# Two blocks of a hybrid network on one core: the rotary turns of an indexer's queries by transfers within SBUF instead of matrix products

## The chip, the cores and the metric

The kernel runs on one core of one Trainium2 chip. The metric is device microseconds (us) of one execution. Five engines work side by side, each through its own instructions in a fixed order: TensorE (PE; its weight loads are listed apart as PEld), VectorE (DVE), ScalarE (ACT), GpSimd (POOL) and SyncE (SP). SP and ACT also start transfers (DMA); the part of an engine that does so is its queue (SPq, ACTq).

## The reference

A sequence of 512 tokens of width 1024 passes through two blocks of two layers each. The change lies in the second block, in both of its layers. There a latent of 256 columns is expanded twice: to 8 attention heads, and to 8 heads of a small "indexer" that decides which 128 of the keys each query may attend to. What the change touches is the rotary turn of the indexer's queries:

```python
def rope(x, positions):
    ...
    x1, x2 = jnp.split(x.astype(jnp.float32), 2, axis=-1)
    return jnp.concatenate([x1 * cos - x2 * sin, x2 * cos + x1 * sin], axis=-1).astype(x.dtype)
...
q_idx = rope((cq @ w_qidx_up).reshape(b_, seq, N_IDX_HEADS, IDX_DIM), positions)
...
idx_logits = jnp.einsum('thd,sd->ths', qib, ki32)
idx_score = jnp.einsum('ths,th->ts', jax.nn.relu(idx_logits), wib)
...
_, sel = lax.top_k(idx_score, n_sel)
```

Beside this attention a layer has a second mixer, an mLSTM with four heads, whose queries and keys go through a short convolution and whose output is gated.

## The kernel before

Activations lie transposed in SBUF: 128 features on the partitions, 512 tokens in a row. Two heads of 64 fill one tile, so the eight indexer heads are four tiles, p = 0 to 3. A rotary turn needs for every partition the value of the partner 32 rows away. `rope2` gets it in one of two ways: by a product with a 128x128 permutation (`swap`) into a PSUM bank `T`, or, when `swap` is None, by four transfers of 32 partitions each (64 KB) from tile to tile, which ACT's queue starts. Then DVE multiplies the partner by the sine (L1270), the tile by the cosine (L1271) and adds (L1275, or L1273 where there is a single output). The attention's own queries and keys (L1527 to L1539) already go by transfers in this kernel. For the indexer's queries the sum is split into a rounded part (ACT, L273) and the rest (DVE, L274), and both feed the score products.

The general products run with weights that are split the same way: a weight unit is loaded from HBM into a `wraw` buffer (L199), ACT casts it to `whi` (L273), DVE makes `wlo` (L274); there are three buffers of each. Product results are in the tiles `mm` (three banks), scores in `S` (two banks).

The stage around the change is the middle of `mixers2`. In program order:
- four times: six products of the latent with `wq` into an `mm` bank (`up`), an ACT copy to a tile `g` (L1382), and the rotary turn;
- the gates of the mLSTM: a chain of small ACT and DVE operations (L1392 to L1409) with two changes of ACT's function table;
- for p = 0 to 3 and three blocks of queries: six score products into two `S` banks, ACT's Relu out of each bank (L1425), and DVE's weighted sum (L1427, L1429). That is 24 Relus a layer;
- the mLSTM loop over four heads (L1459 to L1505), with DVE's top-k (L1284, L1285) in small steps between.

Between these stand jobs: the units of the short convolution (`conv`: 24 products of a weight unit with `h_lat`, then L1340, L1343, L1344). The order on each engine is not that of the program text: a scheduler orders each engine's instructions at build time, by priorities in program order and by its own estimate of when operands are ready. So an operation that it takes to be late lets others pass in front of it, on every engine. At run time each engine keeps this order.

Of the kernel before, what the change touches and what calls it, by code (L numbers as in the profile page):

```python
# [86 lines left out]
class Kern:  # L87
# [1201 lines left out]
    def mixers2(self, l, st, h, gw, cont):  # L1289
# [9 lines left out]
        g = lambda: self.til(G, [P, T], F32, "g")  # L1299
# [59 lines left out]
        def up(w, p):  # L1359
            ps = self.mmbank()  # L1360
            for k in range(2):
                c = slice((2 * p + k) * P, (2 * p + k + 1) * P)
                self.mm3(ps, w[0][:, c], w[1][:, c], cqn[k][0], cqn[k][1], k == 0, k == 1)
            return ps
# [15 lines left out]
        for p in range(4):  # L1380
            x = g()
            A.copy(x, up(wq, p))  # L1382
            q = hl()
            self.rope2(q, x, self.swap, g)
            iq.append(q)

        self.table()
# [24 lines left out]
        for p in range(4):  # L1412
            q = iq[p]
# [45 lines left out]
        for hd in range(4):  # L1459
# [4 lines left out]
            q, k = [self.need(j) for j in j_qk[hd]]  # L1464
# [669 lines left out]
```

## Time and profile before

| | |
|---|---|
| median of 3 runs | 3306.04 us (3303.74 to 3310.87) |
| profiled execution | 3315.37 us, of which the trace spans 3313.6 us |
| PE busy | 3171.0 us, 96% of the span |
| DVE, ACT busy | 2017.3 us (61%), 1355.8 us (41%) |
| granted PE clock, mean | 0.98 |
| the changed stage, layer 0 of block 2 | starts about 1900 us into the span |
| the same stage, layer 1 | starts about 2634 us |

Busy shares are means over the whole span. Inside a stage the engines take other shares, so the stage has to be read by itself. A busy PE in this trace counts a product from its start to its modelled end, and products overlap; how much of PE's time one product takes is read from the starts of the products around it.

### The profile page before, as it was taken

Reading aid. Unit: us, or ns where it says so; the run is one execution under the profiler, and the core shown is the slowest. Engines: PE = TensorE matmul, PEld = TensorE weight load, DVE = VectorE, ACT = ScalarE, POOL = GpSimd, SP = SyncE. Lnnn points to the kernel's source line nnn. Section 1 sums busy time; section 2 is a strip of 40 time slices with the busy share of each in tenths; the row PEclk is TensorE's granted clock in tenths of the full one; section 3 lists DMA queues with packets and bytes.
Section 4 is the critical chain, followed back from the end, with each engine's and each line's share of the span. In section 5 each row is a group of like instructions: output and inputs, shape, how many; then the busy total and the mean of one; then the engine's idle time right before and its main releaser. Section 6 shows DMA issues by size and latency. Waiting matters only on the chain. (4 is left out here: it accounts for less than half of the span.)

```text
span 3313.6 us, 52576 instructions
## 1 busy us (share of the span) xinstructions
PE 3171.0 (96%) x20868; PEld 2697.4 (81%) x20868; DVE 2017.3 (61%) x4147; ACT 1355.8 (41%) x2397; POOL 64.5 (2%) x91
## 2 busy tenths in 40 slices
PE   7899999999999899989999999989999999999999
PEld 5787778888889877778889968778889867778889
DVE  4757557544345756576665798575656797563335
ACT  4554454212122543443224575543325474543334
POOL 0000001000000000010000000000000000000000
PEclk9999999999999999999999999989999999999999
DMA  7443213324243422125554312245655212233235
GB/s 269 161 160 98 72 51 102 115 89 136 75 138 110 134 71 74 50 90 183 198 187 159 124 52 83 71 147 165 205 166 180 96 61 76 75 109 97 101 112 159
DMA packets 141925, 397.43 MB, mean 120 GB/s; under 512 B 29416, under 2 KB 39400, under 8 KB 141680
## 3 DMA queue, kind: packets, MB, share of 16 engines
q1 hardware_dynamic: 137440, 387.76, 36.0%
q10 hardware_dynamic: 4240, 6.31, 0.7%
q8 instruction: 164, 2.69, 0.3%
q14 instruction: 81, 0.66, 0.1%
HBM read 387.70 MB, written 2.11 MB: 118 GB/s over the span
## 5 line engine op out<-in xcount | busy, mean ns | idle before, releaser
L274 DVE TENSOR_TENSOR wlo<-wraw,whi 128x1024 fp32r<-128x1024 f32 (+3 forms) x484 | 568.0, 1177 | 661.8 <-PE mm L81 403.3
L81 PE MATMUL mm<-h_lat,whi 128*128 128x512 f32 (+1 forms) x3888 | 939.9, 387 | 2.1 <-DVE h_lat L368 0.9
L81 PEld LDWEIGHTS mm<-h_lat,whi 128*128 128x128 f32 x3888 | 715.4, 188 | 156.5 <-issue 14.3
L273 ACT CAST whi<-wraw 128x1024 fp32r<-128x1024 f32 (+3 forms) x484 | 488.0, 1013 | 853.7 <-PE mm L81 735.8
L81 PE MATMUL mm<-h_lat,wlo 128*128 128x512 f32 (+1 forms) x1944 | 491.6, 384 | 0.0
L81 PEld LDWEIGHTS mm<-h_lat,wlo 128*128 128x128 f32 x1944 | 363.5, 188 | 72.7 <-issue 2.9
L449 DVE SCALAR_TENSOR_TENSOR macc<-mraw,cst,macc 128x512 f32<-128x512 f32 x280 | 207.2, 750 | 36.3 <-DMA mraw<-wm 32.1
L81 PE MATMUL mm<-ah,whi 128*128 128x256 f32 (+1 forms) x702 | 217.5, 310 | 4.1 <-ACT hc L367 4.1
L81 PE MATMUL mm<-al,whi 128*128 128x256 f32 (+1 forms) x702 | 217.3, 310 | 0.0
L81 PE MATMUL mm<-ah,wlo 128*128 128x256 f32 (+1 forms) x702 | 217.2, 309 | 0.0
L81 PE MATMUL mm<-b,whi 128*128 128x256 f32 (+1 forms) x924 | 181.9, 295 | 0.0
L506 ACT ACTIVATE sb<-sb,least 128x512 f32<-128x512 f32 (+4 forms) x184 | 119.0, 647 | 110.3 <-DVE least L503 100.1
L81 PEld LDWEIGHTS mm<-b,whi 128*128 128x128 f32 x924 | 145.1, 188 | 6.0
L81 PEld LDWEIGHTS mm<-ah,whi 128*128 128x128 f32 x702 | 132.8, 189 | 11.8 <-ACT hc L367 4.2
L81 PEld LDWEIGHTS mm<-ah,wlo 128*128 128x128 f32 x702 | 132.9, 189 | 8.1
L81 PEld LDWEIGHTS mm<-al,whi 128*128 128x128 f32 x702 | 132.8, 189 | 7.4
L81 PE MATMUL mm<-b,wlo 128*128 128x256 f32 (+1 forms) x462 | 136.2, 295 | 0.0
L273 ACT CAST ah<-fx 128x256 fp32r<-128x256 f32 (+1 forms) x77 | 43.0, 559 | 199.3 <-DVE fx L1152 199.3
L81 PE MATMUL mm<-whi,h_lat 128*128 128x256 f32 x640 | 120.5, 289 | 1.8 <-DVE vm L274 1.8
L81 PE MATMUL S<-hc,whi 128*128 128x256 f32 (+1 forms) x768 | 107.5, 283 | 3.9 <-ACT whi L273 3.9
L81 PEld LDWEIGHTS mm<-whi,h_lat 128*128 128x128 f32 x640 | 102.4, 195 | 6.8 <-DVE vm L274 2.4
L81 PE MATMUL S<-h_lat,whi 128*128 128x256 f32 (+1 forms) x448 | 95.7, 302 | 9.4 <-ACT h_lat L367 5.3
(373 smaller groups left out, 5214.9 us busy)
## 6 DMA issues: line engine op xcount, KB each, us to landing
mraw<-wm SPq DMA_DIRECT2D x144, 512.0 KB
wraw<-wgu SPq DMA_DIRECT2D x88, 512.0 KB
wraw<-wgub SPq DMA_DIRECT2D x88, 512.0 KB
wraw<-wA SPq DMA_DIRECT2D x78, 512.0 KB
wraw<-wB SPq DMA_DIRECT2D x54, 512.0 KB
wraw<-wdb SPq DMA_DIRECT2D x56, 448.0 KB
wraw<-wm SPq DMA_DIRECT2D x48, 512.0 KB
wraw<-wd SPq DMA_DIRECT2D x44, 448.0 KB
```

What stands on the lines that cost most here:

```text
L81: return self.tell(self.K.nc.tensor.matmul(*a, **k))
L273: nc.scalar.copy(hi, ps)
L274: nc.vector.tensor_tensor(lo, ps, f32(hi), op=ALU.subtract)
L449: V.scalar_tensor_tensor(acc[v], raw[:, i * 512:(i + 1) * 512], c, acc[v], ALU.mult, ALU.add)
L506: A.activation(x["sb"], x["sb"], AF.Exp, bias=x["init"], scale=-1.0, accum_out=x["sum"])
```

## The change

In the loop over the indexer's four query tiles the argument that chooses the permutation product becomes None, so that the four transfers are made instead. It acts on eight turns: four tiles in each of two layers. The turn of the indexer's key (`swapdup`) stays a product.

```diff
--- before
+++ after
@@ -1381,7 +1381,7 @@
             x = g()
             A.copy(x, up(wq, p))
             q = hl()
-            self.rope2(q, x, self.swap, g)
+            self.rope2(q, x, None, g)
             iq.append(q)
```

With `swap` None the product's place is taken by these lines of `rope2`, and the cosine product is written over the tile itself instead of into a third one:

```python
            for i in range(4):
                j = i ^ 1
                nc.scalar.dma_start(u[32 * i:32 * i + 32], x[32 * j:32 * j + 32])
            pr, w = u, x
```

The scheduler gives a new order. Three places, all in layer 0; layer 1 has the same sequences.

The first is ACT's queue where the turns begin, in the kernel before. COPY is L1382 (tile g from an `up` bank), `kidx` the key's cast, `qh` the cast of a turned query tile, `whi` the cast of a weight unit.

```order
L1382 COPY g_19262<-mm_19263 128x512
L273 CAST kidx_19235<-g_19239 128x512
L1382 COPY g_19282<-mm_19283 128x512
L273 CAST qh_19271<-g_19275 128x512
L273 CAST whi_19651<-wraw_19650 128x1024
L1382 COPY g_19302<-mm_19303 128x512
```

And ACT's queue at the same place with the change:

```order
L1382 COPY g_19262<-mm_19263 128x512
L1265 DMA g_19273<-g_19262 32x512 x2
L273 CAST kidx_19235<-g_19239 128x512
L1265 DMA g_19273<-g_19262 32x512 x2
L273 CAST whi_19655<-wraw_19654 128x1024
L1382 COPY g_19283<-mm_19284 128x512
L1265 DMA g_19294<-g_19283 32x512 x4
L273 CAST qh_19271<-g_19262 128x512
L1382 COPY g_19304<-mm_19305 128x512
L273 CAST whi_19720<-wraw_19719 128x1024
```

The second COPY has moved behind four transfers and behind the cast of a weight unit.

The second place is ACT's queue at the first Relus out of the score banks (L1425), before; L1394 and L1395 are the gate chain's Exp and Ln, ACT_TABLE_LOAD changes the function table.

```order
L273 CAST qh_19331<-g_19335 128x512
L462 ACT_TABLE_LOAD
L1394 ACTIVATE g_19345<-g_19345 4x512
L1425 ACTIVATE g_19372<-S_19364 128x256
L1395 ACTIVATE g_19345<-g_19345 4x512
L1425 ACTIVATE g_19375<-S_19365 128x256
L1425 ACTIVATE g_19386<-S_19378 128x384
L273 CAST whi_19848<-wraw_19847 128x1024
```

With the change, ACT, the same two Relus (S_19368 and S_19369):

```order
L1425 ACTIVATE g_19376<-S_19368 128x256
L273 CAST whi_19917<-wraw_19916 128x1024
L1394 ACT_TABLE_LOAD
L1394 ACTIVATE g_19349<-g_19349 4x512
L273 CAST qh_19334<-g_19325 128x512
L462 ACT_TABLE_LOAD
L1395 ACTIVATE g_19349<-g_19349 4x512
L1425 ACTIVATE g_19379<-S_19369 128x256
L1425 ACTIVATE g_19390<-S_19382 128x384
```

Between the first and the second Relu there are now a weight cast, two table loads, Exp, Ln and the cast of the last query tile; before there was Ln alone.

The third place is PE's queue at the second block of scores. Before, `mm_19495` is the second conv unit of the stage (one of 16 products with `whi`, in the middle of which scores stand), and S the scores:

```order
L81 MATMUL mm_19495<-h_lat_87,whi_19490 128x512
L81 MATMUL S_19378<-kidx_19235,qh_19271 128x384
L81 MATMUL S_19378<-kidx_19236,qh_19271 128x384
L81 MATMUL S_19378<-kidx_19235,qh_19272 128x384
L81 MATMUL mm_19495<-h_lat_88,whi_19490 128x512
L81 MATMUL S_19379<-kidx_19235,qh_19271 128x384
```

With the change, PE, the same scores, now in the third conv unit, `mm_19660`:

```order
L81 MATMUL mm_19660<-h_lat_88,whi_19655 128x512
L81 MATMUL mm_19660<-h_lat_87,wlo_19656 128x512 x2
L81 MATMUL S_19382<-kidx_19235,qh_19271 128x384
L81 MATMUL S_19382<-kidx_19236,qh_19271 128x384
L81 MATMUL S_19382<-kidx_19235,qh_19272 128x384
L81 MATMUL mm_19660<-h_lat_87,wlo_19656 128x512 x6
L81 MATMUL S_19383<-kidx_19235,qh_19271 128x384
```

PE has a whole conv unit more in front of these scores. When it reaches the mLSTM's first products, 50 conv products of this stage are left in its queue; before, 58 were.

## Rows read from the trace of the kernel before

**Rows 1.** The page, part 1: busy time, share of the span, instructions.
```profile
PE 3171.0 (96%) x20868; PEld 2697.4 (81%) x20868; DVE 2017.3 (61%) x4147; ACT 1355.8 (41%) x2397; POOL 64.5 (2%) x91
```

**Rows 2.** Busy time by stretch of layer 0: PE, PEld, DVE, ACT, POOL, PE clock, DMA share, GB/s.
```profile
1900.00:1910.00 10.00, 10.00 (x44) 6.67 (x43) 8.60 (x15) 4.26 (x8) 0.00 (x0) 1.00 0.33 105
1910.00:1920.00 10.00, 10.00 (x42) 7.41 (x40) 8.65 (x13) 6.71 (x11) 0.00 (x0) 1.00 0.25 77
1970.00:1980.00 10.00, 6.41 (x25) 5.12 (x25) 9.90 (x25) 7.27 (x11) 0.00 (x0) 0.67 0.05 13
```

**Rows 3.** Timeline of PE, layer 0: start us, us, what.
```profile
1906.37 0.40 PE L81 MATMUL mm<-cqn,whi 128*128 128x512 f32 x1
1906.61 1.02 PE L81 MATMUL T<-g,swap 128*128 128x512 f32 x2
...
1907.69 0.39 PE L81 MATMUL mm<-cqn,wlo 128*128 128x512 f32 x1
1907.92 0.63 PE L81 MATMUL mm<-cqn,whi 128*128 128x512 f32 x2
1908.39 0.40 PE L81 MATMUL mm<-cqn,wlo 128*128 128x512 f32 x1
1908.72 0.68 PE L81 MATMUL S<-kidx,qh 64*128 64x256 f32 x6
1909.32 1.20 PE L81 MATMUL mm<-h_lat,whi 128*128 128x512 f32 x4
...
1946.03 1.38 PE L81 MATMUL S<-qh,qh 128*128 128x512 f32 x6
```

**Rows 4.** Timeline at an attention turn by transfers (ACT and its queue, then DVE).
```profile
2074.76 0.59 ACT L1527 COPY g<-mm 128x512 f32<-128x512 f32 x1 [2.86 <-PE mm L81]
2075.37 2.44 ACTq L1265 DMA_DIRECT2D g<-g  x4
2077.86 0.40 ACT L506 ACTIVATE sb<-sb,least 128x128 f32<-128x128 f32 x1 [2.52 <-DMA g<-g]
...
2079.25 0.70 DVE L1270 TENSOR_TENSOR g<-g,sinT 128x512 f32<-128x512 f32 x1 [1.45 <-DMA g<-g]
```

**Rows 5.** Timeline of ACT in the changed stage, layer 0.
```profile
1902.41 0.59 ACT L1382 COPY g<-mm 128x512 f32<-128x512 f32 x1 [1.97 <-PE mm L81]
1904.01 0.62 ACT L273 CAST kidx<-g 128x512 fp32r<-128x512 f32 x1 [1.01 <-DVE g L1275]
...
1908.59 1.05 ACT L273 CAST whi<-wraw 128x1024 fp32r<-128x1024 f32 x1 [0.61 <-PE mm L81]
1909.54 0.58 ACT L1382 COPY g<-mm 128x512 f32<-128x512 f32 x1
...
1918.03 1.28 ACT L462 ACT_TABLE_LOAD   x1
1919.32 0.63 ACT L1394 ACTIVATE g<-g 4x512 f32<-4x512 f32 x1
1919.86 0.36 ACT L1425 ACTIVATE g<-S 128x256 f32<-128x256 f32 x1
```

**Rows 6.** Timeline of PE: eight products with wlo, and a block of scores.
```profile
1947.71 1.98 PE L81 MATMUL mm<-h_lat,wlo 128*128 128x512 f32 x8
1949.52 0.84 PE L81 MATMUL mm<-h_lat,whi 128*128 128x512 f32 x3
...
1920.27 0.79 PE L81 MATMUL S<-kidx,qh 64*128 64x384 f32 x3
1920.99 0.51 PE L81 MATMUL mm<-h_lat,whi 128*128 128x512 f32 x1
```

**Rows 7.** PE after its longest gap of the layer, and stretches around gaps (columns as Rows 2).
```profile
1974.38 0.80 PE L81 MATMUL S<-qh,qh 128*128 128x256 f32 x2 [3.59 <-DVE w L1483]
...
1974.40:1980.00 5.60, 5.60 (x20) 4.56 (x21) 5.60 (x13) 5.52 (x7) 0.00 (x0) 0.50 0.01 3
2074.00:2076.00 2.00, 0.72 (x4) 0.26 (x2) 1.30 (x2) 0.59 (x1) 0.00 (x0) 1.00 0.02 5
```

## Prediction

> **What bounds the kernel now.** I read the page first: PE is busy 96% of the span, so a product taken away can be worth its own time [rows 1]. Then the stage itself, in stretches of 10 us: when the turns run, PE is busy 10.00 of 10.00 us in both stretches, while DVE has 1.4 us to spare in each and ACT 5.7 and 3.3 us [rows 2]. So at the place of the change PE sets the pace and ACT looks free. Further on it is different: at 1970 to 1980 DVE is busy 9.90 us and PE 6.41 [rows 2]. There DVE sets the pace, so a delay of either one early in the layer is hardly won back later. Last I read the timelines of PE and ACT row by row, because the order in which ACT now works is another one.
>
> **What goes.** One permutation product costs PE 0.85 us: between the start of the `up` product ahead of it (1906.37) and that of the second product behind it (1907.69) are 1.32 us, and two products of that kind at their pitch (1907.69 to 1907.92) take 0.23 each [rows 3]. Eight of them are 8 x 0.85 = 6.8 us, 3.4 a layer, at a place where PE never idles. DVE's work stays: four operations a turn, which now read SBUF instead of PSUM.
>
> **What comes, on ACT.** A turn by transfers is seen in the attention: the copy ends at 2075.35, ACT's queue starts four transfers in 2.44 us, and the next activation begins at 2077.86, after 2.52 us without one [rows 4]. DVE gets its operand at 2079.25, that is 1.44 us after the last of the four was started (2075.37 + 2.44 = 2077.81). So a turn takes 2.4 us of ACT's order, and its operand is there 3.9 us after the copy, where the product gave it in about 2. Four turns are 9.8 us of ACT's queue per layer. Spread out, they would fit in ACT's spare time. What matters is what is queued behind them.
>
> **First new wait (a).** In the new order the copy of the second `up` bank stands behind four transfers and behind a weight cast that overwrites the weights which the last `up` products still read. Without the two swaps that lie ahead of it, the last `up` product starts at 1908.39 - 1.70 = 1906.69, and the weights are free at 1906.9. The cast takes 1.05 us, but the copy starts 0.95 after it [rows 5], at 1907.85, and is done at 1908.43. The first conv product needs the bank that this copy empties. PE is through with the `up` products at 1906.95, so it waits until about 1908.55: 1.6 us. The transfers of the first turn are long started by then (the first copy ends at 1903.0, two starts, the key's cast, two starts: 1906.1), so here it is the place of the copy that costs, not the transfers.
>
> **Second new wait (b), the larger one.** From 1908.55 PE has 24 + 24 + 16 conv products and 6 scores before the third unit's `whi` is free. At a pitch of 0.23 us (eight products from 1947.71 to 1949.52 [rows 6]) and 0.60 for the scores (1908.72 to 1909.32 [rows 3]) this ends at 1908.55 + 14.7 + 0.6 = 1923.85. Only then can ACT make the cast of the next unit, which stands ahead of the second Relu. Behind the cast come a table load, Exp, a query's cast, a table load and Ln. By the starts in [rows 5] that is 0.95 + 1.29 + 0.54 + 0.62 + 1.29 + 0.54, and 0.36 for the Relu: 5.6 us, to 1929.5. Meanwhile PE has 8 products (1.8) and one block of scores (1920.27 to 1920.99, 0.7 [rows 6]) and is at 1926.4 when it needs the bank that this Relu empties. It idles for 3.1 us. The transfers of the last turns lie earlier (started by about 1920.2), so they are not on this path unless they land 4 us later than in [rows 4].
>
> **What follows to the end of the scores.** Now 22 Relus are left, and PE has hardly any conv products to put between. From 1929.5 ACT has those 22 (six of 0.36 and sixteen wider ones, for which I take 0.47 and 0.58, the latter that of a copy of 512 columns [rows 5]: 2.2 + 3.8 + 4.6 = 10.6 us), and of the conv and the gates two L1340, two Silus, a table load and three casts, about 7 us by the same pitches: 18 us, to 1947.5 if ACT never waits, with two banks more like 1950. I take 1950 for the mLSTM's first product. Before it came at 1946.03 [rows 3]. That is 4 us late, but 50 conv products are left instead of 58: 8 x 0.23 = 1.8 us to the good. Net +2.2 us a layer, the 3.4 us saved already counted; with 1947.5 it would be -0.3.
>
> **The clock.** The longest gap of the layer now, 3.59 us, is followed by granted 0.50 (1.2 GHz) from 1974.4 to 1980 [rows 7]. A stretch with 0.72 us of work in two stayed at 1.00. Gap (b) with 3.1 us lies between, nearer to the first, and the stretch behind it is thin. So I take the clock to fall: such a stretch, 5.6 us at half speed, costs 2.8 us of work if PE has work, and nothing if ACT sets the pace throughout. Bounds 0 and 5 a layer (5: twice such a stretch, as in the scores and again in the conv unit behind them, less what waits on ACT anyway); taken 2.8. The Trainium skill ("TensorE: Matmul & The Clock Gate", section "Why this matters for your kernels") warns of idle gaps between bursts of products, because they bring the clock down to its lower level; the trace agrees with the 0.50 behind its gap. By that rule the sum is the one below. If gap (b) is too short to bring the clock down, the sum is 2 x 2.2 = 4.4 us.
>
> Of the table loads another page of the Trainium skill speaks: "ScalarE: Activation LUTs", section "What ACT_TABLE_LOAD costs", adds a drain to each, about 2.66 us in all. The rows do not show it: 1918.03 to 1919.32 is 1.29 us [rows 5]. By the page gap (b) would be some 2.7 us longer a layer; I stay with the row.
>
> **The sum.** 2.2 + 2.8 = 5.0 us a layer, 10 us in all. The profiled execution took 3315.37 us (span 3313.6), 9.3 above the median of 3306.04; its 3325.4 is 3316 against the median. A change of 0.2% (6.6 us) is about the least that a measurement here tells from none.
>
> **The rivals.**
> - *The saved product time comes through*: faster by 6.8 us, 3299. For it: PE is full at this place, and transfers in the attention do serve. It decides at one point: the second Relu must come before PE needs its bank at 1926.4, so ACT's chain behind the third unit must take under 2.6 us instead of 5.6, and the copy of (a) must come 1.6 us earlier. Against it: both lie in the order of ACT's queue, and durations come from rows. Chance 0.15.
> - *Late, but nearly made good*: gaps as worked out, no fall of the clock, or DVE's spare 1.4 us per 10 [rows 2] takes up the rest. -0.3 to +2.2 a layer: 3305.4 to 3310.4; it gives 3309. Chance 0.30.
> - *Worse*: the clock stays low through the thin stretch (5 us), and the old 3.59 us gap in the mLSTM grows because DVE, too, starts its top-k later (2 us more). 2.2 + 5 + 2 = 9.2 a layer: 3324. For it: DVE at 9.90 of 10 just there [rows 2]. Chance 0.13.
> - That the change doesn't do what it says is excluded: the order shows the transfers and no swap.
>
> **Chances and range.** The forecast (3311 to 3321, +2.5 to +7.5 a layer) has 0.42. Faster by over 0.2% is the first rival: 0.15. Within 0.2% (3299.4 to 3312.6) are nearly all of the second and the lower end of the forecast: 0.33. Slower: 0.52. The range for 8 in 10 reaches down to 3298, into the first rival, and up to 3326, leaving out that rival's lower half and the end of the worst.
>
> **What would show it.** In the new profile: PE gaps of about 1.6 us before the first conv unit of the stage and of about 3 us before the second block of scores, the latter put down to L1425; the second Relu at about 1929, where the first stands at 1919.86 now [rows 5]; granted clock below 1.00 between 1928 and 1945; the mLSTM's first product near 1950; no operation of DVE that waits over 2 us for a transfer at the moment PE stands. All of it twice. It is wrong if the second Relu comes before 1926, if the scores end before 1947 with the clock at 1.00, or if a transfer lands so late that DVE becomes the first to wait.

## The result, and the profile after

The changed kernel takes 3340.59 us (median of 4 runs, 3338.92 to 3349.04) against 3307.1 beside it: ratio 1.0099, 95% interval [1.0086, 1.0112]. It is slower by 33 us; 10 were forecast, and the range ended at 3326. The first part of the page and the granted clock over 40 equal slices, in tenths (layer 0 begins in slice 23):

```profile
PE 3179.9 (95%) x20852; PEld 2706.2 (81%) x20852; DVE 2017.5 (60%) x4147; ACT 1363.3 (41%) x2403; POOL 65.9 (2%) x91
...
PEclk8999999999999999999999989989999989999999
```

Set against [rows 1] this tells little: the 16 product instructions are gone, the other engines do the same work. The stages tell more. Layer 0 is cut at the same five events: first `up` product, first mLSTM product, last mLSTM score, the transpose of R, last product of the attention. Columns as in [rows 2]; before first:

```profile
1900.36:1946.03 45.67, 45.30 (x200) 29.86 (x199) 40.56 (x67) 28.86 (x51) 0.00 (x0) 1.00 0.21 70
1946.03:2021.15 75.12, 70.08 (x357) 55.12 (x356) 71.86 (x183) 51.99 (x85) 0.00 (x0) 0.95 0.22 71
2021.15:2035.49 14.34, 14.34 (x71) 10.49 (x71) 14.34 (x32) 9.48 (x15) 0.00 (x0) 1.00 0.16 48
2035.49:2168.32 132.83, 128.22 (x845) 103.19 (x843) 78.67 (x268) 60.87 (x157) 0.00 (x0) 1.00 0.26 80
```

And after:

```profile
1898.39:1954.49 56.10, 50.70 (x200) 35.97 (x199) 41.03 (x66) 31.07 (x53) 0.00 (x0) 0.88 0.25 76
1954.49:2030.48 75.99, 70.16 (x360) 54.99 (x358) 72.85 (x186) 54.23 (x86) 0.00 (x0) 0.96 0.22 70
2030.48:2046.61 16.13, 12.90 (x62) 9.36 (x61) 16.03 (x35) 9.27 (x16) 0.00 (x0) 0.96 0.21 66
2046.61:2182.24 135.63, 130.79 (x843) 105.46 (x843) 76.33 (x263) 60.78 (x157) 0.00 (x0) 0.98 0.25 76
```

The layer is 15.9 us longer. Idle PE time (first figure less the second) rises from 10.0 to 19.3 us. Work lost to a low clock (one less the mean clock, times the length; an estimate, since idle time at a low clock is counted in both) rises from 3.8 to about 13. So 9.3 + 9.3 is lost. The layer is only 15.9 us longer, which leaves 2.7 us for the product time, of which 3.4 was forecast. Layer 1, cut alike, is 17.2 us longer. Together that is 33 us, the difference of the medians. The two profiled spans differ by 26 only: outside these stretches the trace of before is 7 us the longer, 3.0 of them in one wait for the weights `wo` that the trace after doesn't have.

PE in layer 0:

```profile
1906.48 3.90 PE L81 MATMUL mm<-h_lat,whi 128*128 128x512 f32 x16 [1.38 <-ACT g L1382]
...
1928.25 3.15 PE L81 MATMUL S<-kidx,qh 64*128 64x384 f32 x12 [3.03 <-ACT g L1425]
...
1954.49 1.39 PE L81 MATMUL S<-qh,qh 128*128 128x512 f32 x6
```

Waits (a) and (b) are there, 1.38 and 3.03 us, put down to the second copy and to the second Relu; layer 1 has the same two. ACT shows the chain ahead of that Relu:

```profile
1921.95 0.36 ACT L1425 ACTIVATE g<-S 128x256 f32<-128x256 f32 x1
1922.49 1.06 ACT L273 CAST whi<-wraw 128x1024 fp32r<-128x1024 f32 x1 [0.19 <-PE mm L81]
1923.56 1.28 ACT L1394 ACT_TABLE_LOAD   x1
1924.86 0.63 ACT L1394 ACTIVATE g<-g 4x512 f32<-4x512 f32 x1
...
1927.84 0.72 ACT L1425 ACTIVATE g<-S 128x256 f32<-128x256 f32 x2
```

From cast to Relu it takes 5.35 us; the sum from [rows 5] had 5.23. But behind it the clock stays low for much longer than forecast:

```profile
1920.00:1930.00 10.00, 6.97 (x29) 4.80 (x28) 7.77 (x13) 8.27 (x13) 0.00 (x0) 0.97 0.31 105
1930.00:1940.00 10.00, 9.59 (x32) 7.11 (x32) 10.00 (x19) 6.57 (x12) 0.00 (x0) 0.50 0.00 1
1940.00:1950.00 10.00, 9.82 (x35) 6.19 (x34) 6.05 (x11) 5.59 (x13) 0.00 (x0) 0.85 0.00 1
```

And at the end of the mLSTM there are waits that the prediction doesn't have. PE there before, and then after:

```profile
2029.69 0.22 PE L81 MATMUL T<-wl,dsel 128*4 128x128 f32 x1
2029.75 0.45 PE L81 MATMUL mm<-h_lat,whi 128*128 128x512 f32 x1
2030.04 1.97 PE L81 MATMUL mm<-h_lat,wlo 128*128 128x512 f32 x8
2031.97 1.02 PE L81 MATMUL T<-g,ld 128*4 128x512 f32 x2
```

```profile
2041.37 0.33 PE L81 MATMUL o<-wl,vm 128*128 128x128 f32 x1 [1.18 <-DVE wl L274]
...
2041.65 0.22 PE L81 MATMUL T<-wl,dsel 128*4 128x128 f32 x1
2042.98 1.02 PE L81 MATMUL T<-g,ld 128*4 128x512 f32 x2 [1.12 <-ACT g L1503]
2044.89 0.50 PE L81 MATMUL mm<-whi,h_lat 128*128 128x256 f32 x2 [0.89 <-ACT g L1457]
```

Before, nine convolution products lie between the last products into `o` and the sum of squares (`T<-g`), which has to wait for ACT's copy and square of `o`. Six products of the attention's queries (`mm<-cqn`) follow behind it. After, all of these stand ahead of the last products into `o`, and nothing is left to cover the waits.

### The profile page after: what moved, and what is told of

The parts are those of the page before. It is cut to its first block, busy times and chain, and to the rows that moved or that the text cites. A ratio compares the mean times of both kernels' runs of the same rounds, so it can differ in the third digit from the quotient of the medians.

```text
span 3339.6 us, 52598 instructions
## 1 busy us (share of the span) xinstructions
PE 3179.9 (95%) x20852; PEld 2706.2 (81%) x20852; DVE 2017.5 (60%) x4147; ACT 1363.3 (41%) x2403; POOL 65.9 (2%) x91
```

## The experiments

The first four take the change apart. Here and below, ratios are to runs of the kernel before on the same chip.

**kept_busy** fills wait (b). `first` is the output of the first Relu.

```diff
+                        if p == 0 and b == 2 and part == 0 and i == 1:
+                            pd = self.bank(self.psT, "T")
+                            for _ in range(8):
+                                self.pe.matmul(pd[:, :256], self.ident, first[:, :256], start=True, stop=True)
```

> The changed kernel with eight extra products of the identity with the first Relu's output (256 columns, result not used) between the first and the second block of scores, so that TensorE has something to do while it waits for the second Relu. Nothing else is changed. Theory (the wait of 3.0 us brings the clock down, and 13.7 and 17.1 us at half speed behind it cost about 7 and 8 us of work): the wait shrinks below 1 us, the low stretches at 1929 and 2673 are gone, and the time falls by 10 to 16 us, to 3324 to 3331 us. Rival (the clock falls there for another reason, or work behind it waits for ScalarE anyway): 3337 to 3344 us.

Measured 3342.68 us, 1.0106 [1.0093, 1.0120]: the theory fell.

```profile
1921.81 3.72 PE L81 MATMUL T<-g,ident 128*128 128x256 f32 x16
...
1930.80 0.62 PE L81 MATMUL S<-kidx,qh 64*128 64x256 f32 x3 [0.72 <-ACT g L1429]
```

And its stretches:

```profile
1930.00:1940.00 10.00, 7.78 (x29) 5.33 (x29) 10.00 (x19) 6.92 (x12) 0.00 (x0) 0.70 0.15 52
1940.00:1950.00 10.00, 9.82 (x33) 6.06 (x31) 6.06 (x11) 4.94 (x11) 0.00 (x0) 0.78 0.01 2
```

No wait in this stretch is over 0.9 us now (together PE is idle for 2.2 us from 1930 to 1940), and the clock falls all the same, later, among scores that stand alone. The first mLSTM product comes at 1954.77.

**gates_first** moves the lines of the gate chain (L1392 to L1409, with the call ahead of them) to a place ahead of the loop over the four tiles.

> The changed kernel with the mLSTM's gate chain (its table loads, Exp and Ln) ahead of the four turns in the program, transfers as in the change. Theory (what costs is that the second Relu stands behind table loads, and what follows from it): no table load is left between the Relus, the wait before the second block of scores is under 1 us, no low clock there, and the time is 3300 to 3320 us. Rival (the transfers themselves cost, by ScalarE's queue or by late operands): 3333 us or more.

3327.24 us, 1.0063 [1.0051, 1.0076]: between the two. No table load stands between the first Relus any more, but PE waits 4.8 us for the gate chain's `irow` before the scores, and the low clock follows there (0.66 from 1910 to 1920); among the scores themselves it is 1.00 in layer 0.

**half_first** and **swap_in_place**:

```diff
-            self.rope2(q, x, None, g)
+            self.rope2(q, x, None if p < 2 else self.swap, g)
```

```diff
-            pr, w = self.bank(self.psT, "T"), tmp()
+            pr, w = self.bank(self.psT, "T"), x if over else tmp()
...
-            self.rope2(q, x, self.swap, g)
+            self.rope2(q, x, self.swap, g, over=True)
```

> Transfers for the tiles p = 0 and 1 only, products for p = 2 and 3, in both layers. The order at the first Relus is that of the kernel before (Ln alone between them). Theory (the order at the second Relu decides): wait of 1.4 us at the second copy, but none at the second block of scores; half of the products are saved (3.4 us): 3303 to 3309 us. Rival (each transfer costs its share): half of the loss, 3320 to 3327 us.

> The kernel before with one part of the change alone: the product stays, and the cosine product is written over the tile. Theory (the loss comes from the place of the transfers and what they push back): no change beyond 0.3%, 3300 to 3315 us. Rival (the loss comes from the two buffers per turn, by which other operations get buffers in another order): most of the loss, 3325 us or more.

half_first: 3324.99 us, 1.0055 [1.0043, 1.0066], the rival's number, although it has no wait over 1.0 us for a Relu. Its waits at the end of the mLSTM (1.2, 1.1 and 0.9 us) are the changed kernel's. swap_in_place: 3321.78 us, 1.0043 [1.0031, 1.0056], nearly half of the loss without one transfer. Its first mLSTM product comes at 1946.07, as before, with 76 convolution products of the stage done by then in place of 86. Of its waits at the end of the mLSTM two are those of the changed kernel, the third is shorter (0.5 for 1.18):

```profile
PE T L81 <- ACT g L1503: 1.1, 1, 1.1
PE mm L81 <- ACT g L1457: 0.9, 1, 0.9
PE o L81 <- DVE wl L274: 0.5, 1, 0.5
```

As in the changed kernel, no convolution product stands behind the last products into `o`; before there were nine. So a part of the loss comes without transfers, with the order that the scheduler gives. The next four followed from this.

**dense_scores** adds, to kept_busy, behind four blocks of scores:

```diff
+                if (p, b) in ((0, 3), (1, 1), (1, 2), (1, 3)):
+                    pd = self.bank(self.psT, "T")
+                    for _ in range(4):
+                        self.pe.matmul(pd, q[0][:, c], kidx[0], start=True, stop=True)
```

> As kept_busy, and four more extra products of all 128 rows and 512 columns (0.23 us each at full clock, results not used) behind each of the next four blocks of scores, p = 0 and 1, in both layers. kept_busy filled the wait of 3 us, and the clock fell all the same, 5 us later, among scores that use 64 rows with waits under 1 us between. Theory (a stretch of scores alone, with or without a wait ahead of it, brings the clock down): no low clock between 1925 and 1945, and the stretch, 3.7 us of extra products included, is no longer than in the changed kernel: the first product of the mLSTM within 2 us of 1954.5, time 3330 to 3343 us. Rival (the clock falls whatever TensorE does there): the low stretch stays, the extra products cost their time twice, 3348 us or more.

3341.83 us, 1.0100 [1.0086, 1.0114]. The low stretch is gone:

```profile
1930.00:1940.00 10.00, 10.00 (x47) 6.22 (x47) 7.76 (x14) 7.41 (x14) 0.00 (x0) 1.00 0.00 1
1940.00:1950.00 10.00, 9.82 (x41) 5.57 (x41) 9.39 (x17) 5.72 (x11) 0.00 (x0) 1.00 0.17 55
```

From the first `up` to the first mLSTM product it takes 54.82 us in place of 56.10, although 7.4 us of products were added (3.72, and 16 of 0.23). Two convolution products fewer (92 for 94) stand in this stretch, 0.5 us. So idle time and low clock were worth some 8 us here, an estimate, but the added work eats them up.

**third_tile** (transfers with `w` a third tile), **pool_queue** (the 32 transfers on `nc.gpsimd`), **gates_first_swap** (the move of gates_first in the kernel before):

```diff
-            pr, w = u, x
+            pr, w = u, (tmp() if third else x)
```

```diff
-                nc.scalar.dma_start(u[32 * i:32 * i + 32], x[32 * j:32 * j + 32])
+                (eng or nc.scalar).dma_start(u[32 * i:32 * i + 32], x[32 * j:32 * j + 32])
```

> The changed kernel with the transfers, but with a third tile per turn for the cosine product, as the kernel before has it. swap_in_place lost 15 us with no transfer at all, through another order. If that loss is a part of the loss of the change (the two add up), this kernel loses 33 - 15 = 18 us: 3319 to 3328 us. Rival (each of the two gives an order of its own, and the losses don't add): the first Relu stands behind both table loads here, its wait alone is 3 us or more, and the time is 3333 us or more.

> The changed kernel with the same transfers started by GpSimd's queue in place of ScalarE's, for the indexer's tiles only. ScalarE has no DMA starts in this stage, and its copies stand before the weight casts. Theory (the loss comes from the order of ScalarE's queue): the wait at the second copy is gone, the wait at the second block of scores is at most 2 us, and the time is 3305 to 3325 us. Rival (the transfers themselves are late for VectorE, whoever starts them): VectorE waits over 2 us for a transfer while TensorE stands, 3330 us or more.

> The kernel before with the mLSTM's gate chain moved ahead of the four turns, products kept: no transfer, only another order. gates_first (the same move with transfers) took 3327 us. Theory (the stage loses by any order that takes conv products from the end of the mLSTM or delays the top-k; transfers are not needed for it): 3312 to 3325 us. Rival (transfers make the loss of gates_first): 3300 to 3310 us.

third_tile: 3341.55 us, 1.0099 [1.0085, 1.0113], the rival's; the losses don't add, each order has its own (wait for a Relu 4.2 us). pool_queue: 3331.21 us, 1.0071 [1.0057, 1.0084]: the time is the rival's, but neither account holds. VectorE waits for no transfer, PE for no Relu longer than 0.7 us and not for the second copy at all, and still the clock is 0.54 from 1930 to 1940. gates_first_swap: 3318.85 us, 1.0033 [1.0020, 1.0045], as expected, with no transfer: up to the mLSTM it loses nothing (44.22 us for 45.68, with 79 convolution products done by then in place of 86), and at the mLSTM's end PE is idle for 2.5 us a layer, where before it never was.

**cover_end** gives the mLSTM's last block a priority:

```diff
+                with (self.tc.high_priority(offset=40) if hd == 3 and j == 3 else ExitStack()):
...
```

> The changed kernel with a higher priority for the last column block of the last mLSTM head, so that two convolution products and three of the attention's query products stand behind the last products into o instead of ahead of them, and three more behind the sum of squares; up to there the order on TensorE is the changed kernel's. Theory (at the end of the mLSTM the changed kernel has lost the products that covered its last waits, 3.2 us idle a layer, and a low clock follows): these waits fall below 1.5 us, the low clock at 2045 and 2793 is gone, and the time is 5 to 11 us below the changed kernel's, 3329 to 3335 us. Rival (the end waits for VectorE's top-k anyway, so a wait moves to the next product): 3337 to 3343 us.

3331.94 us, 1.0067 [1.0055, 1.0079]: as the theory had it. PE at the same place:

```profile
2037.51 0.22 PE L81 MATMUL T<-wl,dsel 128*4 128x128 f32 x1
2037.57 0.67 PE L81 MATMUL mm<-h_lat,wlo 128*128 128x512 f32 x2
2038.08 0.63 PE L81 MATMUL mm<-cqn,whi 128*128 128x512 f32 x2
2038.54 0.40 PE L81 MATMUL mm<-cqn,wlo 128*128 128x512 f32 x1
2038.87 1.02 PE L81 MATMUL T<-g,ld 128*4 128x512 f32 x2
```

Five products moved behind the last `o`, and three behind the sum of squares, are worth some 9 us of the 33. PE is idle for 0.05 us there, and the low clock at 2045 and 2793 is gone. Ahead of the first mLSTM product stand 94 convolution products, as in the changed kernel; before there were 86.

**dense_cover** (both edits) and **sp_queue** (the transfers on `nc.sync`):

> dense_scores and cover_end together: extra products among the scores, and the order of cover_end at the end of the mLSTM. dense_scores brought the mLSTM's first product 3.6 us forward in layer 0, and its time was that of the changed kernel, 3342. Theory (two losses at two places, which add): 7 to 14 us below the changed kernel, 3326 to 3333 us. Rival (what is won among the scores is lost again in the mLSTM, where VectorE sets the pace): as cover_end, within 3 us.

> The changed kernel with the indexer's transfers started by SyncE's queue, between its weight loads. Both table loads of the gate chain stand ahead of the first Relu, one more behind the second. Theory (the order of ScalarE decides, and the end of the mLSTM loses its cover as in every new order so far): no wait at the second copy, a wait of up to 3 us at the first Relus, 3 us at the end of the mLSTM: 3322 to 3336 us. Rival (SyncE's weight loads are held up behind transfers that wait for their tile, TensorE waits for weights): 3340 us or more.

dense_cover: 3329.93 us, 1.0066 [1.0053, 1.0080], in the ranges of both: the extra products cost what they save. sp_queue: 3330.91 us, 1.0065 [1.0050, 1.0079], as expected.

What was still open is whether the place of the convolution products decides. **interleaved** pins them between the scores, two at a time; **early_relus** and **early_swap** give the scores a priority.

```diff
+            if self.pinned:
+                yield 2
...
+        for _ in range(1):
+            self.tick()
...
+                self.pinned = True
...
-            self.tick()
+                self.work(2)
+                self.pinned = False
```

```diff
+            with (self.tc.high_priority(offset=30) if p < 4 else ExitStack()):
                 q = iq[p]
                 for b in range(1, 4):
...
```

> The changed kernel (transfers) with the order on TensorE pinned in the scores: two products of a convolution unit stand between one block of scores and the next, so that the convolution products can't all run ahead of the scores. At the end of the mLSTM nine convolution products stand again between the last products into o and the sum of squares, and six query products behind it, as in the kernel before. Theory (with transfers the convolution products are used up before the scores; these then run alone, wait for Relus, and the clock falls; and the end of the mLSTM is bare): no low clock of over 7 us in the scores, no wait of over 1 us at the mLSTM's end; what is left is the start of the scores and ScalarE's table loads: 3308 to 3325 us. Rival (the late turns or ScalarE's table loads set the scores' end, with convolution products between them or not): 3330 us or more.

> cover_end with a priority for the scores, their Relus and sums that lets the Relus pass the gate chain: two Relus stand ahead of the first table load, three between the two, none waits for the whole chain. The convolution products all stand ahead of the scores, of which 36 run in a row; the end of the mLSTM has the cover of the kernel before. Theory (what counts is that the scores run alone, not the table loads among the Relus): the wait for the second Relu is under 1.5 us, the low clock stays, and the first product of the mLSTM comes within 3 us of 1953: 3320 to 3334 us. Rival (the table loads between the Relus were the loss): the mLSTM starts 5 us earlier or more, under 3318 us.

> The kernel before (products, no transfer) with a smaller priority for the scores. The convolution products stand between the scores as in the kernel before, and the end of the mLSTM is word for word that of the kernel before. Theory (the loss hangs on these two features of the order): another order that has both doesn't lose: 3300 to 3313 us. Rival (every order but the given one loses some 10 us, as swap_in_place and gates_first_swap did): 3315 us or more.

interleaved: 3344.09 us, 1.0107 [1.0094, 1.0121], the rival's. The end of the mLSTM is covered (14.34 us, as before), but the new order puts both table loads ahead of the first Relu:

```profile
1913.12 1.28 ACT L1398 ACT_TABLE_LOAD   x1
...
1915.57 1.28 ACT L466 ACT_TABLE_LOAD   x1
1916.86 0.63 ACT L1399 ACTIVATE g<-g 4x512 f32<-4x512 f32 x1
1917.40 0.62 ACT L1432 ACTIVATE g<-S 128x256 f32<-128x256 f32 x2
```

PE then:

```profile
1917.81 1.59 PE L81 MATMUL S<-kidx,qh 64*128 64x384 f32 x6 [5.27 <-ACT g L1432]
```

PE waits 5.27 us, and for two copies 4.0 more. The clock falls behind these waits too (0.55 from 1920 to 1930), although at most six scores stand together. early_relus (offset 80, and the edit of cover_end): 3327.6 us, 1.0057 [1.0043, 1.0071]. That is the theory's time, but not by its path: PE waits up to 2.3 us for a Relu, and the mLSTM begins at 1949.2, 5 us earlier than in the changed kernel, as the rival had it, with the clock at 0.50 from 1940 to 1950. That is not won: only 72 convolution products stand ahead of the mLSTM in place of 94, and the 22 others (22 x 0.23 = 5.1 us) come later, so that from there to the mLSTM's last score it takes 81 us in place of 76. early_swap, the kernel before with the second edit alone: 3303.7 us, 0.9984 [0.9976, 0.9993], faster than either kernel. PE there, at the second block of scores and on:

```profile
1913.67 1.05 PE L81 MATMUL S<-kidx,qh 64*128 64x384 f32 x6
1914.65 1.85 PE L81 MATMUL mm<-h_lat,whi 128*128 128x512 f32 x7
1916.43 1.65 PE L81 MATMUL S<-kidx,qh 64*128 64x512 f32 x6
1918.02 0.73 PE L81 MATMUL mm<-h_lat,whi 128*128 128x512 f32 x2
1918.68 0.72 PE L81 MATMUL S<-kidx,qh 64*128 64x256 f32 x6
```

Convolution products stand between the blocks, here seven and two; there is no wait, and the clock is 1.00.

**one_turn** is early_swap with `None if p == 0 else self.swap` and the edit of cover_end; **early_swap_more** is early_swap with offset 80.

> early_swap, with transfers for the first of the four tiles alone and the priority of cover_end at the end of the mLSTM. Convolution products stand between the scores as in early_swap, and five query and convolution products stand behind the last products into o. Theory (the transfers are harmless where the order keeps the convolution products between the scores and some behind the last products into o): no low clock in the scores, waits at the mLSTM's end under 1.5 us, 3300 to 3312 us. Rival (transfers lose their share, a quarter of 33 us, whatever the order): 3311 us or more, with new waits at the turns or low clock in the scores.

> early_swap with a larger priority for the scores (80 in place of 30); products, no transfer. Both features of the order are kept. Theory (as for early_swap, which took 3304 us): 3298 to 3310 us. Rival (the larger priority starves the mLSTM's convolution units, which come later): 3312 us or more.

one_turn: 3315.76 us, 1.0020 [1.0011, 1.0029], outside the theory's range and in the rival's. The scores have no wait and the clock is 1.00 from 1900 to 1960. What is left are the wait for the copy behind the transfers (1.4 us), a longer one in the mLSTM (4.4 us for L1485, 3.4 in early_swap) and 0.8 us for a copy in the attention (L1562). It takes 12 us more than early_swap. How much of that is the turn's own is not shown: one_turn also has the edit of cover_end, and early_swap with that edit alone was not run. No order tried here made a transfer free. early_swap_more: 3303.85 us, 0.9986 [0.9977, 0.9995], like early_swap.

## Why the prediction was wrong

- **Waits (a) and (b)**: right in place, cause and size, 1.38 and 3.03 us for 1.6 and 3.1. The transfers start and land in time, as said; the copy and the Relu stand too far back in ACT's order.
- **The first mLSTM product** ("I take 1950"): it came at 1954.49, and the stage began 2.0 us earlier. The stage is 10.4 us longer up to there; the sum had 4 us and 2.8 for the clock, 3.6 too little.
- **The clock, "taken 2.8", bounds 0 and 5 a layer**: this term was too small, and its upper bound too. Up to the first mLSTM product the low clock took 12% of 56.10 us, 6.7 us of work, and in layer 1 more (57.00 us at 0.85, 8.6 us). The stretch after the old 3.59 us gap [rows 7] was the wrong measure. kept_busy shows that the gap alone doesn't decide: without it the clock falls too. dense_scores shows that it stays at 1.00 when other products stand among the scores; as they also take away the short waits there (PE busy 10.00 of 10 us from 1930 to 1940, 7.78 in kept_busy), it isn't shown which of the two counts. By the Trainium skill ("TensorE: Matmul & The Clock Gate", section "Why this matters for your kernels") idle gaps between bursts bring the clock down. kept_busy agrees only in part, since its waits there are 0.9 us at most and the clock fell to its lower level of 1.2 GHz.
- **"8 x 0.23 = 1.8 us to the good"**: this step failed in kind, and it is the larger miss (7.3 us a layer). I counted the products done early, and the sum put new waits behind the first mLSTM product at nothing. Behind it the layer was to win 1.8 us and lost 5.5 (0.9, 1.8 and 2.8). In the new order nothing stands behind the last products into `o`, and 3.2 us of waits lie bare at the end of the mLSTM; a low clock follows. cover_end, which puts products behind them again, takes 9 us less in both layers together. It is tempting to say that the convolution products done early (66 ahead of the second block of scores, before 39) were missing here. The runs speak against it: cover_end does as many ahead of the mLSTM and has its cover, while swap_in_place, which does fewer than the kernel before (76 for 86), has none. What decides is where the scheduler puts the last of them; why it puts them there is not shown.
- **The rival that the mLSTM's old gap grows**: it did, by 0.8 us (4.4 for 3.59).
- **The saved product time** shows as what is left over (2.7 us in layer 0 for 3.4), not by a run of its own. It is small beside the 18.6 us lost.

What stays open: how the loss of up to 10.4 us ahead of the mLSTM divides between scores that stand alone and ACT's table loads. interleaved mended the one and worsened the other, early_relus the reverse, and neither won. gates_first had both right in layer 0, but paid ahead of them, with the 4.8 us for `irow` and the low clock behind it. That both have to be right is consistent with early_swap and one_turn, but no version with all four turns by transfers had them right without a new wait. half_first together with the edit of cover_end was not run. The changed kernel's Exp starts 1.30 us after its table load does (1923.56 to 1924.86). The drain that the Trainium skill ("ScalarE: Activation LUTs", section "What ACT_TABLE_LOAD costs") adds to a load is not seen in it.

## What to carry to other kernels

When an operation moves off the engine that is full, ask what the scheduler will put in its place: in a new order a wait far behind the edit can lose the products that covered it. Count for each later wait which products lie over it in the new order, and not only the waits near the edit. Compare times up to an event that no work has crossed: a stage that starts earlier may only have got more of the products, as the mLSTM did in early_relus. And try the order alone: here a priority on one loop, with nothing else changed, beat both kernels, while two harmless edits without any transfer lost 10 and 15 us.

## What the hardware showed that was not expected

The same wait can bring the clock down or not. In kept_busy PE waits about 2.0 us for the same turn in both layers, with the same products around it. Layer 0, then layer 1:

```profile
2090.00:2092.00 2.00, 1.75 (x13) 1.46 (x14) 0.71 (x5) 0.63 (x3) 0.00 (x0) 0.77 0.42 102
2092.00:2094.00 2.00, 2.00 (x6) 1.62 (x6) 1.25 (x2) 0.78 (x3) 0.00 (x0) 0.50 0.12 29
...
2836.00:2838.00 2.00, 1.53 (x14) 1.20 (x15) 0.92 (x5) 0.41 (x3) 0.00 (x0) 1.00 0.40 98
2838.00:2840.00 2.00, 2.00 (x10) 1.65 (x9) 0.97 (x2) 1.52 (x5) 0.00 (x0) 1.00 0.17 41
```

Behind the one the clock is 0.50, behind the other 1.00. The changed kernel has such a fall behind the same wait in both layers (3.4 us at 0.50 from 2089.74 and from 2837.26, 1.7 us of work each), the kernel before, with the same wait, in neither. So 3.4 of the 33 us may be no doing of the change.

The clock can also fall while PE is nearly full. In swap_in_place the longest wait from 1918 to 1932 is 0.2 us; layer 0, then the same place in layer 1:

```profile
1920.00:1930.00 10.00, 9.81 (x36) 5.61 (x36) 8.34 (x15) 6.33 (x12) 0.00 (x0) 0.83 0.08 30
2655.63:2665.63 10.00, 9.81 (x44) 5.79 (x43) 8.95 (x16) 6.36 (x12) 0.00 (x0) 1.00 0.09 34
```
